# Weights of both output projections and of keys and values, 192 bytes further into their buffers

## The chip, the cores and the metric

The kernel runs on one core of a Trainium2 chip. The metric is the device time of one execution in microseconds. Before the change the median of three runs is 975.04 us (974.99 to 975.18). Engines are called PE (TensorE; PEld is its loading of the stationary operand), DVE (VectorE), ACT (ScalarE), POOL (GpSimd) and SP (SyncE, which issues most DMAs).

## What is computed

A decoder trunk of two layers over 256 tokens of width 2048, all in float32. Layer 0 is a Mamba-2 mixer, layer 1 is attention over a sliding window of 128 tokens with 32 heads, 4 heads of keys and values, and a sink per head. Cut to what matters here:

```python
# layer 0
zxbcdt = x @ w_in                         # 2048 -> 10304 columns
...                                       # conv, silu, state-space scan, gate, rms norm -> y (256 x 4096)
x = layernorm(ALPHA * x + y @ w_out)      # output projection, 4096 -> 2048
# layer 1
kv = x @ kv_w + kv_b                      # 2048 -> 512, keys and values
proj = x @ w_in                           # 2048 -> 4096, queries and gates
...                                       # rotary, scores, softmax with sink, values -> o (256 x 2048)
x = layernorm(ALPHA * x + (o * silu(gate)) @ w_out)   # output projection, 2048 -> 2048
```

## The kernel before

Nearly all of the work is these matrix products, and each weight is used once. Weights come from memory in **units** of 128 x 2048 float32 (1 MB), each as two halves of 1024 columns, through six buffers `wr` (L169). A product in float32 is made of three products in the faster type float32r: ACT copies a half into a high part `wh` (L178), which rounds it, and DVE subtracts that from the original and stores the rest as the low part `wl` (L181). Activations are split in the same way into `xH` and `xL`, `x1H` and `x1L`, `yH` and `yL`, `oH` and `oL`. A product is then high x high + high x low + low x high, three matmuls into the same accumulator.

Units are used in two ways.

- **Narrow** (`narrow`, `q_block`, `gate_block`, through `mac`, L265): the weights are the stationary operand, 128 x 128 at a time, and 256 tokens of activations move. A unit is 16 blocks x 3 = 48 matmuls of 256 columns. The input projection of layer 0 (`in_wa`, 80 units) and the queries and gates of layer 1 (`in_wq`, `in_wg`, 32 units) run so.
- **Wide** (`out_unit`, L339, and `x_stat`, L1052): the activations are the stationary operand, and 512 columns of weights move. A unit is 2 halves of the tokens x 4 blocks x 3 = 24 matmuls of 512 columns. The output projections (`in_wo`, 32 units, and `in_wb`, 16 units) and keys and values (`in_wkv`, 4 units) run so. In the very last unit the second half of the tokens goes in two pieces of 256 columns.

**Where the parts lie in their buffers.** There are four buffers `wh` and four `wl`, each of 2112 float32 a partition: 2048 for the unit, and 64 (256 bytes) to spare. A table of places, `(offset, first block, last block)` in float32, says where in the buffer the 16 blocks stand: `WHOLE` puts all at 0; `BROKEN` and `BROKEN2`, for the queries and gates, put most blocks at a multiple of 256 bytes plus 64, and the first one or two at 0 (`wh`) or 192 (`wl`) bytes. `split_half` writes there, and the matmuls read from there. The activations of layer 0 (`Split`) lie 192 bytes past a multiple of 256, but for their first block; `yH`, `yL`, `x1H`, `x1L`, `oH` and `oL` begin at a multiple of 256 bytes, and so does every 128 x 128 block in them. The program puts each of the buffers named here at an address that is a multiple of 256.

**Order.** `srcs` lists the units in the order of their use: the input blocks of `SEQ`, with units of the output projection let in by `OUT_AT`, then the rest of that projection, keys and values, and the units of `B_ORDER`. `next_unit` loads `AHEAD = 2` units beyond the one in use: SP issues their DMAs as `wr` buffers come free, ACT and DVE split them as `wh` and `wl` buffers come free. Other work of ACT and DVE (convolution, scan, softmax, the evictions of accumulators, L348 and its neighbours) stands between the splits on the same engines.

Of the kernel before, what the change touches and what calls it, by code (L numbers as in the profile page):

```python
# [20 lines left out]
KT = D // P  # L21
# [76 lines left out]
def trunk(ctx: ExitStack, tc: tile.TileContext, A: dict, out: bass.AP, dbg=None):  # L98
# [51 lines left out]

    WHOLE = [(0, 0, KT)]
    BROKEN = [[(0, 0, 1), (144, 1, KT)], [(1968, 0, 1), (16, 1, KT)]]
    BROKEN2 = [[(0, 0, 2), (272, 2, KT)], [(1840, 0, 2), (16, 2, KT)]]

    def new_unit(places):
# [29 lines left out]
    def load_unit(src, places, pin=False, pin_h=False, n=(1, 1)):  # L185
        u = new_unit(places)
        raws = [load_half(u, src, c, n[c]) for c in range(2)]
        for c in range(2):
            split_half(u, raws[c], c, pin, pin_h)
        return u  # L190
# [24 lines left out]


    srcs = []

    def wo_srcs(name, j):
        return [A[name][j * 4 + i] for i in range(4)]  # L220

    for n, (g, b) in enumerate(SEQ):
        srcs.append(A["wa"][g * 10 + (BLOCKS0.index(b) if g == 0 else b)])
        if n in OUT_AT:
            g, i = OUT_AT[n]
            srcs.append(A["wo"][g * 4 + i])
    srcs += [A["wo"][(NG - 2) * 4 + i] for i in (1, 2, 3)]
    srcs += wo_srcs("wo", NG - 1) + [A["wkv"][i] for i in range(4)]
    places = {}
    for what, j in B_ORDER:  # L230
        if what in "gq":

            places.update({len(srcs) + i: BROKEN2 if (what, i, j) == ("g", 1, 0) else BROKEN for i in range(4)})
        srcs += wo_srcs({"q": "wq", "g": "wg", "o": "wb"}[what], j)
# [3 lines left out]
    def load_next(n, pin=False, pin_h=True):  # L238
        for _ in range(n):
            if len(units) == 4:  # L240
                nc.sync.dma_start(cc[:], A["cc"])
            for i in [i for i, n in enumerate(XK_AT) if n == len(units)]:

                v = xr[:, i % 2, i // 2 * 1024 : i // 2 * 1024 + 1024]
                tc.keep_in_program_order(
                    nc.sync.dma_start(v, A["xk"][:, i % 2, i // 2 * 1024 : i // 2 * 1024 + 1024])
                )


            i = len(units)  # L250
            units.append(
                load_unit(
                    srcs[i], places.get(i, [WHOLE, WHOLE]), pin, pin and pin_h,
                    [2 if 2 * i + c >= 2 * len(srcs) - SPLIT else 1 for c in range(2)],
                )
            )

    def next_unit(behind=False):
        load_next(min(used[0] + 1 + AHEAD, len(srcs)) - len(units), behind, not behind)
        used[0] += 1  # L260
        return units[used[0] - 1]
# [535 lines left out]
    first_ps = first_products()  # L797
    dt_first, dt_second = make_dt(first_ps[0])
    load_next(1, True)
    dt_begun = dt_first()  # L800
    load_next(1, True)
    dt_sums = dt_second()
    load_next(1, True)
# [780 lines left out]
```

## Time and profile before

| what | value |
|---|---|
| median of the runs | 975.04 us |
| profiled execution, first to last instruction (its span) | 973.8 us |
| the median's distance to that span | 1.24 us |
| PE busy, matmul records | 965.5 us, 7332 |
| PEld busy | 892.0 us |
| DVE busy | 786.6 us |
| ACT busy | 671.4 us |
| DMA queue of SP, share of the 16 engines' span | 59.1% |
| granted TensorE clock | 1.000 |

The profile gives one time for the profiled execution, its span; the times of the runs include what lies around it. A matmul's record is longer than the spacing of matmuls: a wide one's is 390 ns, a narrow one's 277 ns, and they overlap. What a matmul costs is read from start to start, or from merged runs in the chain of waits (start, length, count). A line of the windows view has a stretch, its length, the busy time of an engine with the number of its instructions, the granted clock, the share of DMA time and the bytes per second.

### The profile page before, as it was taken

Reading aid. Unit: us, or ns where it says so; the run is one execution under the profiler, and the core shown is the slowest. Engines: PE = TensorE matmul, PEld = TensorE weight load, DVE = VectorE, ACT = ScalarE, POOL = GpSimd, SP = SyncE. Lnnn points to the kernel's source line nnn. Section 1 sums busy time; section 2 is a strip of 40 time slices with the busy share of each in tenths; the row PEclk is TensorE's granted clock in tenths of the full one; section 3 lists DMA queues with packets and bytes.
Section 4 is the critical chain, followed back from the end, with each engine's and each line's share of the span. In section 5 each row is a group of like instructions: output and inputs, shape, how many; then the busy total and the mean of one; then the engine's idle time right before and its main releaser. Section 6 shows DMA issues by size and latency. Waiting matters only on the chain.

```text
span 973.8 us, 18857 instructions
## 1 busy us (share of the span) xinstructions
PE 965.5 (99%) x7332; PEld 892.0 (92%) x7332; DVE 786.6 (81%) x1217; ACT 671.4 (69%) x1282; POOL 119.1 (12%) x202
## 2 busy tenths in 40 slices
PE   9999999999999999999999999999999999999998
PEld 8999989998999999999899899888999988898976
DVE  7978898896977877787797687889977769778778
ACT  7675884884785686487477579467777776884772
POOL 0000403102110310310300121411000000000002
PEclk9999999999999999999999999999999999999999
DMA  9689467676656666576476654568654545456542
GB/s 359 237 290 337 147 216 228 212 230 203 218 192 220 205 205 206 167 237 213 152 250 203 216 178 155 187 190 265 193 174 158 185 138 186 153 177 213 205 143 86
DMA packets 61273, 197.90 MB, mean 203 GB/s; under 512 B 6800, under 2 KB 11328, under 8 KB 60928
## 3 DMA queue, kind: packets, MB, share of 16 engines
q1 hardware_dynamic: 58528, 188.53, 59.1%
q0 software_dynamic: 2048, 7.65, 2.4%
q8 instruction: 57, 0.93, 0.4%
q10 hardware_dynamic: 608, 0.52, 0.2%
q14 instruction: 32, 0.26, 0.1%
HBM read 194.45 MB, written 2.23 MB: 202 GB/s over the span
## 4 chain that ended last, share of the span: by engine, by line
PE 75%; DVE 10%; ACT 6%; DMA 5%; issue 3%; SPq 1%; DVEq 0%; ACTq 0%
PE mm L265 48%; PE mm L339 20%; DVE wl L181 4%; DMA wr<-in_wa 2%; PE mm L1052 2%; PE ax L670 2%; ACT wh L178 2%; DMA wr<-in_wb 1%; ACT p L1248 1%; DMA xr<-in_first 1%; DVE cv L510 1%; ACT e L566 1%; ACT ptw L1281 1%; ACT pt L1281 0%; DMA rscr<-f 0%
## 5 line engine op out<-in xcount | busy, mean ns | idle before, releaser
L181 DVE TENSOR_TENSOR wl<-wr,wh 128x1024 fp32r<-128x1024 f32 (+2 forms) x354 | 391.5, 1126 | 87.8 <-ACT wh L178 86.0
L178 ACT ACTIVATE wh<-wr 128x1024 fp32r<-128x1024 f32 (+2 forms) x354 | 332.9, 974 | 95.9 <-PE mm L265 50.9
L265 PE MATMUL mm<-xH,wh 128*128 128x256 f32 x1280 | 354.6, 277 | 0.1
L265 PE MATMUL mm<-xH,wl 128*128 128x256 f32 x1280 | 353.8, 276 | 0.0
L265 PE MATMUL mm<-xL,wh 128*128 128x256 f32 x1280 | 353.7, 276 | 0.0
L265 PEld LDWEIGHTS mm<-xH,wh 128*128 128x128 f32 x1280 | 240.3, 188 | 2.3 <-issue 1.0
L265 PEld LDWEIGHTS mm<-xL,wh 128*128 128x128 f32 x1280 | 240.4, 188 | 1.0
L265 PEld LDWEIGHTS mm<-xH,wl 128*128 128x128 f32 x1280 | 240.3, 188 | 0.1
L265 PE MATMUL mm<-x1H,wh 128*128 128x256 f32 x512 | 142.2, 278 | 2.1 <-DVE sg L1186 2.1
L265 PE MATMUL mm<-x1L,wh 128*128 128x256 f32 x512 | 141.6, 277 | 0.0
L265 PE MATMUL mm<-x1H,wl 128*128 128x256 f32 x512 | 141.5, 276 | 0.0
L339 PE MATMUL mm<-wh,yH 128*128 128x512 f32 x256 | 100.8, 394 | 0.1
L339 PE MATMUL mm<-wh,yL 128*128 128x512 f32 x256 | 99.8, 390 | 0.0
L339 PE MATMUL mm<-wl,yH 128*128 128x512 f32 x256 | 99.7, 390 | 0.0
L265 PEld LDWEIGHTS mm<-x1H,wh 128*128 128x128 f32 x512 | 96.1, 188 | 3.6 <-DVE sg L1186 2.4
L265 PEld LDWEIGHTS mm<-x1L,wh 128*128 128x128 f32 x512 | 96.2, 188 | 0.1
L265 PEld LDWEIGHTS mm<-x1H,wl 128*128 128x128 f32 x512 | 96.2, 188 | 0.0
L510 DVE SCALAR_TENSOR_TENSOR cv<-mm,pc,cv 128x255 f32<-128x255 f32 x144 | 68.4, 476 | 4.6 <-ACT cv L508 2.5
L686 POOL TENSOR_TENSOR yz<-yz,z 128x256 f32<-128x256 f32 x32 | 26.7, 843 | 259.2 <-DVE yz L681 259.2
L339 PEld LDWEIGHTS mm<-wl,yH 128*128 128x128 f32 x256 | 48.1, 188 | 10.3
L339 PEld LDWEIGHTS mm<-wh,yH 128*128 128x128 f32 x256 | 48.1, 188 | 9.7 <-issue 0.3
L339 PEld LDWEIGHTS mm<-wh,yL 128*128 128x128 f32 x256 | 48.1, 188 | 9.0
(247 smaller groups left out, 1262.8 us busy)
## 6 DMA issues: line engine op xcount, KB each, us to landing
wr<-in_wa SPq DMA_DIRECT2D x154, 512.0 KB, 5.2
wr<-in_wo SPq DMA_DIRECT2D x64, 512.0 KB, 4.4
wr<-in_wq SPq DMA_DIRECT2D x32, 512.0 KB, 4.4
wr<-in_wg SPq DMA_DIRECT2D x31, 512.0 KB, 4.8
wr<-in_wb SPq DMA_DIRECT2D x16, 512.0 KB, 4.0
wr<-in_wb SPq DMA_DIRECT2D x32, 256.0 KB, 4.3
rb<-rscr SPq DMA_DIRECT2D x11, 512.0 KB, 5.4
wr<-in_wkv SPq DMA_DIRECT2D x8, 512.0 KB, 5.7
```

What stands on the lines that cost most here:

```text
L178: m = nc.scalar.activation(h[:, sl], v, AF.Copy)
L181: m = nc.vector.tensor_tensor(l[:, sl], v, h[:, sl].bitcast(F32), ALU.subtract)
L265: m = nc.tensor.matmul(ps, a, b, start=first and i == 0, stop=last and i == 2)
L339: pinned(nc.tensor.matmul(ps, a[:, k, hs], (u.h, u.l)[l][:, ks], start=n == 0 and add is None, stop=n == 11), pin)
L510: nc.vector.scalar_tensor_tensor(a[:, sft:], ps[:, : S - sft], w(3 - sft), a[:, sft:], ALU.mult, ALU.add)
L566: m = nc.scalar.activation(e[:, h, cols], rb[:, h, c * P :], AF.Relu, scale=-1.0, bias=rtk[:, c, h0 + h : h0 + h + 1])
L670: nc.tensor.matmul(ps[64 * r : 64 * r + 64, cols], st.xd[:, c, i, 64 * r : 64 * r + 64], e[:, 256:] if c else e[:, :256], start=c == 0, st ...
L686: nc.gpsimd.tensor_tensor(v, v, st.z[i][:], ALU.mult)
L1052: m = nc.tensor.matmul(ps[:], (x1H, x1L, x1H)[i][:, kk, hs], (u.h, u.h, u.l)[i][:, ks], start=(kk, i) == (0, 0), stop=ui == 3 and (k, i) = ...
L1248: nc.scalar.activation(byhead[:, r], byhead[:, r], AF.Exp, bias=ng[:, r : r + 1], accum_out=rs[:, r : r + 1])
L1281: nc.scalar.copy(to[32 * c : 32 * c + 32].rearrange("p r a -> p (r a)"), src[32 * i : 32 * i + 32, cc_].rearrange("p r b -> p (r b)"),)
```

## The change

A new table of places, `ASIDE`, puts all 16 blocks of both parts at offset 48, which is 192 bytes. The loop that lists the units notes in `stood` the positions of the units of the input projection. A unit which is neither noted there nor has a place in `places` (queries and gates) now gets `ASIDE` in place of `WHOLE`: the units of both output projections and of keys and values. 48 + 2048 = 2096 float32 fit into a buffer's 2112. Nothing else is changed; the sequence of instructions on every engine, and what each waits for, is the same in both programs.

```diff
     WHOLE = [(0, 0, KT)]
     BROKEN = [[(0, 0, 1), (144, 1, KT)], [(1968, 0, 1), (16, 1, KT)]]
+    ASIDE = [[(48, 0, KT)], [(48, 0, KT)]]
     BROKEN2 = [[(0, 0, 2), (272, 2, KT)], [(1840, 0, 2), (16, 2, KT)]]
...
     srcs = []
+    stood = set()
...
     for n, (g, b) in enumerate(SEQ):
+        stood.add(len(srcs))
         srcs.append(A["wa"][g * 10 + (BLOCKS0.index(b) if g == 0 else b)])
...
                 load_unit(
-                    srcs[i], places.get(i, [WHOLE, WHOLE]), pin, pin and pin_h,
+                    srcs[i], places.get(i, [WHOLE, WHOLE] if i in stood else ASIDE), pin, pin and pin_h,
                     [2 if 2 * i + c >= 2 * len(srcs) - SPLIT else 1 for c in range(2)],
```

## The prediction

> **What bounds the kernel now.** I read the head of the page first, then its chain of work that ended last.
>
> ```profile
> span 973.8 us, 18857 instructions
> PE 965.5 (99%) x7332; PEld 892.0 (92%) x7332; DVE 786.6 (81%) x1217; ACT 671.4 (69%) x1282; POOL 119.1 (12%) x202
> PE 75%; DVE 10%; ACT 6%; DMA 5%; issue 3%; SPq 1%; DVEq 0%; ACTq 0%
> ```
>
> PE's 99% says little, because matmul records overlap. The third line says more: for three quarters of the span the chain runs through PE itself. The question is therefore what one matmul costs PE, and where in the program PE sets the pace.
>
> The change touches only "wide" matmuls: a stationary block of activations (128x128) and 512 columns of weights as the moving operand. They stand at L339 (both output projections) and L1052 (keys and values). The windows view, restricted to L339, counts them by stretch (columns: stretch, its length, PE busy and the number of matmuls, granted clock, DMA share, GB/s); the last row is the same view for L1052 over the whole span.
>
> ```profile
> 0.00:130.40 130.40, 11.34 (x48) 1.00 0.77 269
> 130.40:784.00 653.60, 168.89 (x720) 1.00 0.63 202
> 784.00:835.60 51.60, 22.59 (x96) 1.00 0.51 160
> 835.60:900.00 64.40, 22.24 (x96) 1.00 0.58 187
> 900.00:953.00 53.00, 32.93 (x140) 1.00 0.46 160
> 953.00:973.80 20.80, 12.42 (x64) 1.00 0.27 101
> 0.00:973.80 973.80, 22.28 (x96) 1.00 0.62 203
> ```
>
> That is 1164 + 96 = 1260 wide matmuls, all at a granted clock of 1.00. I cut the stretches where the chain changes hands. The chain view's summary line for each of the first five stretches, in order:
>
> ```profile
> by line: DMA wr<-in_wa 17.1%; DVE wl L181 15.2%; issue 11.7%; DMA xr<-in_first 6.3%; DVE cv L510 5.7%; ACT e L566 5.2%; ACT wh L178 3.9%; DMA rscr<-f 3.6%; SPq L206 3.5%; ACT e L573 3.2%; DVE yz L681 3.0%; DVE yL L701 2.1%; DVE e L614 1.6%;
> by line: PE mm L265 66.0%; PE mm L339 25.2%; PE mm L1052 3.3%; PE ax L670 2.9%; PE ax L607 0.5%; PE ax L983 0.5%; PE ax L1220 0.4%; PE ax L1213 0.3%; PE ax L608 0.2%; PE mm L1342 0.2%; PE ax L1328 0.2%; PE mm L1349 0.1%; DVE z L600 0.1%; AC
> by line: DVE wl L181 16.6%; issue 13.8%; ACT p L1248 11.1%; ACT wh L178 8.2%; ACT ptw L1281 7.9%; DVE xr L346 4.8%; DVE sm L1242 4.4%; ACT pte L1281 2.9%; DVE z L1262 2.9%; DVE sw L1151 2.9%; DVE o L1316 2.5%; DVE qT L1154 2.4%; DVE oL L135
> by line: PE mm L265 60.2%; PE mm L339 34.2%; PE ax L1213 1.7%; PE mm L1328 1.6%; PE ax L1342 1.3%; PE ax L1349 0.9%; issue 0.1%
> by line: DMA wr<-in_wb 20.5%; DVE wl L181 18.5%; issue 14.7%; ACT wh L178 11.6%; ACT pt L1281 6.9%; ACT p L1248 5.4%; DVE z L1262 4.7%; DVE xr L350 3.4%; DVE p L1255 2.4%; ACT p L1233 2.2%; ACT ptw L1281 1.5%; DVE sg L1186 1.3%; DVE st L946
> ```
>
> In the second and fourth stretch nothing but PE stands in the chain; a nanosecond taken off a matmul there comes off the span. In the first, third and fifth the chain goes through DVE, ACT and loads while PE keeps just ahead of them; PE time saved there turns into a wait. After 953 us the chain is PE again, until the last matmul:
>
> ```profile
> 953.05 10.82 PE mm L339 x52
> ```
>
> **What a matmul costs, and what address has to do with it.** All times below are from start to start, since the record of one matmul (about 390 ns for a wide one) covers the next one's beginning. I call "distance" the byte address at which the moving operand begins, minus that of the stationary one, modulo 256. Every buffer that these matmuls read begins at a multiple of 256 bytes, so distances follow from the offsets in the code: 0 for all wide matmuls now (weights at 0, activations at 0), 192 for the narrow matmuls (256 columns) of L265, in the first layer because the activations lie 192 bytes in, in the second because the weights lie 64 bytes in (0 - 64 = 192). Merged runs in the chain view (start, length, count):
>
> ```profile
> 349.09 5.45 PE mm L339 x24
> 354.54 10.91 PE mm L265 x96
> 321.86 27.23 PE mm L265 x240
> 677.56 38.19 PE mm L265 x336
> ```
>
> A wide matmul takes 5.45 / 24 = 227 ns. A narrow one takes 27.23 / 240 = 113.5 ns in the first layer and 38.19 / 336 = 113.7 ns in the second. Half the columns take half the time, so this alone could be a plain rate, with nothing to gain. The end of the kernel decides against that: there L339 itself runs pieces of 256 columns, still at distance 0. From the timeline of PE:
>
> ```profile
> 955.25 0.39 PE L339 MATMUL mm<-wl,oH 128*128 128x512 f32 x1
> ...
> 962.05 0.39 PE L339 MATMUL mm<-wl,oH 128*128 128x512 f32 x1
> ...
> 963.95 0.28 PE L339 MATMUL mm<-wh,oH 128*128 128x256 f32 x1
> ...
> 965.27 0.28 PE L339 MATMUL mm<-wl,oH 128*128 128x256 f32 x1
> ```
>
> Wide: 31 matmuls, 30 intervals in 6.80 us, 226.7 ns each. Pieces of 256 at distance 0: 12 matmuls, 11 intervals in 1.32 us, 120.0 ns each, 6.5 ns more than the narrow ones at distance 192. So 256 further columns cost 226.7 - 120.0 = 106.7 ns, and each matmul has a fixed part of 120.0 - 106.7 = 13.3 ns at distance 0. At distance 192 the fixed part is 113.5 - 106.7 = 6.8 ns. The same step shows once more where a unit of the second layer begins: its first products stand at distance 0 or 64, the later ones at 192.
>
> ```profile
> 677.40 0.28 PE L265 MATMUL mm<-x1H,wh 128*128 128x256 f32 x1
> 677.51 0.28 PE L265 MATMUL mm<-x1L,wh 128*128 128x256 f32 x1
> 677.64 0.28 PE L265 MATMUL mm<-x1H,wl 128*128 128x256 f32 x1
> 677.75 0.28 PE L265 MATMUL mm<-x1H,wh 128*128 128x256 f32 x1
> ```
>
> These three take 350 ns together, 117 each, against the 113.7 above. I read it this way: while one matmul streams, PE already loads the next stationary block, both read the same partitions, and when their addresses run along together one of them is held up.
>
> [...]
>
> **The change, part by part.** The order of instructions on all five engines, and what each waits for, is the same before and after; no instruction, DMA or wait is added or taken away, so there is no queue to go past. What differs, in 52 units of weights (32 and 16 of the two output projections, 4 of keys and values), is where ACT (L178) and DVE (L181) write the two parts, and where PE reads them.
>
> - The split on ACT and DVE: the groups view by shape has 896-column pieces, written 64 bytes in, beside whole halves of 1024, of which nine in ten are written at 0.
>
> ```profile
> L181 DVE TENSOR_TENSOR wl<-wr,wh 128x1024 fp32r<-128x1024 f32 x290 | 350.0, 1224 | 74.5 <-ACT wh L178 72.8
> L181 DVE TENSOR_TENSOR wl<-wr,wh 128x896 fp32r<-128x896 f32 x31 | 33.6, 1083 | 3.1 <-ACT wh L178 3.0
> L178 ACT ACTIVATE wh<-wr 128x896 fp32r<-128x896 f32 x31 | 29.2, 942 | 0.0
> ```
>
>  1083 / 896 = 1.21 and 1224 / 1024 = 1.20 ns a column on DVE: no cost of the place is to be seen. I put it at nothing. If a wide unit's split did get slower, its cover is PE's 24 matmuls, 5.45 us a unit, against two DVE splits of 1.22 us; in the third and fifth stretch there is no cover and each 0.1 us would show.
> - The wide matmuls: their distance becomes 192, that of the narrow ones. I expect the fixed part to fall from 13.3 to 6.8 ns, 6.5 ns a matmul, 226.7 to 220.2 ns. Nothing in the trace has 512 columns at distance 192, so this is carried over from 256. The bounds: no gain, if in a wide matmul the loading has so much time that it gives way (0), and 13.3 ns, if the whole fixed part goes. I take 6.5 because distance 0 cost the 256- and the 512-column matmuls of L339 the same fixed 13.3 ns, so length does not seem to matter.
> - What of it reaches the end: 720 + 96 + 96 + 64 = 976 matmuls stand on PE's chain (second and fourth stretch, L1052, the end), 976 x 6.5 = 6.3 us. The other 284 (48 + 96 + 140) would save 1.8 us, which I count as lost: in the third stretch PE ends up waiting for DVE anyway,
>
> ```profile
> 835.64 0.39 PE L265 MATMUL mm<-x1H,wh 128*128 128x256 f32 x1 [2.07 <-DVE sg L1186]
> ```
>
>  and saving 96 x 6.5 = 0.6 us there makes these 2.07 us longer. If all were kept, the gain would be 8.2 us.
> - Entering and leaving wide units: PE's rhythm changes over a few matmuls. On entry, from the timeline:
>
> ```profile
> 381.65 0.39 PE L339 MATMUL mm<-wh,yH 128*128 128x512 f32 x1
> 381.88 0.40 PE L339 MATMUL mm<-wh,yL 128*128 128x512 f32 x1
> 382.11 0.39 PE L339 MATMUL mm<-wl,yH 128*128 128x512 f32 x1
> 382.34 0.39 PE L339 MATMUL mm<-wh,yH 128*128 128x512 f32 x1
> ```
>
>  690 ns for three, 10 above three times 226.7. After a wide unit the run at 354.54 took 10.91 / 96 = 113.65 ns a matmul, 0.15 x 96 = 14 ns above the long run's rate. Some 30 blocks of wide work have both edges: 30 x 24 ns = 0.7 us, which may go or double. I take 0 and keep 0.7 us on both sides.
> - Covers: a faster unit asks for 1 MB of weights in 24 x 220.2 = 5.28 us in place of 5.44. ACT and DVE each hold two splits for it and DVE two evictions besides (745 ns each by the row below), 2 x 1.22 + 2 x 0.75 = 3.9 us, and the DMA share in that stretch is 0.63. Nothing there becomes the bound.
>
> ```profile
> L348 DVE SCALAR_TENSOR_TENSOR xr<-mm,r,xr 128x512 f32<-128x512 f32 x64 | 47.0, 745 | 9.7 <-POOL r L744 4.8 <-PE mm L339 4.7 <-ACT r L742 0.3
> ```
>
> Sum: 973.8 - 6.3 = 967.5 us for the profiled span. The median of the runs, 975.04, is 1.24 us above that execution's span; with the same 1.24 the forecast is **968.7 us**. With the edges and with all or fewer of the matmuls counted, this case's own range is 966.2 (975.0 - 8.2 - 0.7, rounded) to 970.7.
>
> **The rivals.**
>
> *No change, 975.0.* In a wide matmul the stationary load has 227 ns for a job that the narrow ones do in 113; it could simply give way at a collision, and what costs a wide matmul its 13.3 ns could be something that the address does not touch. For it: half the columns at distance 192 take exactly half the time, which a plain rate would explain too, with the 120.0 ns a matter of short matmuls alone. Against it: the coincidence of 13.3 ns would then be chance.
>
> *Slower, 981.3.* Two readers that run at different speeds can lock into a worse rhythm as well as a better one. That a wide matmul can be slower than 226.7 ns is in the rows at 381.65: 230 ns each right after a narrow unit. If the offset that suits 256 columns leaves the two out of step at 512, so that the stream is held up once more for each stationary load, at the price of one such hold-up above (6.5 ns), the 976 matmuls on PE's chain cost 6.3 us: 975.0 + 6.3 = 981.3. The place is every wide unit; it decides from the point at which the fixed part at distance 192 is above 13.3 ns. Against it: at 256 columns the same two distances go the other way, in thousands of narrow matmuls.
>
> *Much faster, 962.0.* The whole fixed part goes: 13.3 x 976 = 13.0 us. For it speaks only that the narrow 6.8 ns could be bound by the load and not by the stream, and in a wide matmul the load has time. [...]
>
> **How the numbers follow.** Forecast 0.62, no change 0.21, slower 0.12, much faster 0.05. A measurement of this kernel tells about 0.2% from nothing, 1.95 us; forecast and much faster are both beyond it, so faster 0.67, same 0.21, slower 0.12. The range goes from 966.0 to 975.3: it holds the forecast's own 966.2 to 970.7 and the case of no change, and leaves out the slower case and the much faster one, 0.17.
>
> **What would show it.** In the profile of the changed kernel: merged runs of L339 x24 at 5.28 us in place of 5.45; the 256-column pieces at the end at 113.5 in place of 120.0 ns; L265 runs, and the means of L178 and L181, as before; the wait at L265 for DVE (2.07 us) longer by some 0.6 us and new waits of PE in the third and fifth stretch. The forecast is wrong if wide runs stay at 5.45 us (no change), if they grow (slower), or if they shrink and the span does not, which would put a load or a split at the end of the second stretch's chain.

## The result and the profile after

| | before | changed | ratio |
|---|---|---|---|
| median of the runs | 975.11 us (974.99 to 975.46, 4 runs) | 986.89 us (986.02 to 987.3, 4 runs) | 1.0118 [1.0104, 1.0133] |
| span of the profiled execution | 973.8 us | 985.5 us | |

The change costs 11.8 us; the forecast was a gain of 6.3 us. The edits add three lines, so L265 is now L268, L339 is L342, L1052 is L1055, and L178 and L181 are L179 and L182.

The page of the changed kernel, its head and the first line of its chain of waits:

```profile
span 985.5 us, 18857 instructions
PE 978.2 (99%) x7332; PEld 900.1 (91%) x7332; DVE 788.2 (80%) x1217; ACT 671.9 (68%) x1282; POOL 119.3 (12%) x202
PE 94%; DVE 3%; ACT 2%; issue 1%; DVEq 0%; ACTq 0%
```

The instructions are the same in number, and DVE, ACT and POOL work as long as before (786.6, 671.4 and 119.1 us there); the time is PE's, whose share of the chain of the whole span goes from 75% to 94%.

The chain view of the changed kernel at the beginning of the second stretch (start, length, what, count), to be held against the prediction's rows of 5.45, 10.91 and 27.23 us:

```profile
144.81 5.79 PE mm L342 x24
150.60 28.27 PE mm L268 x240
178.87 0.43 PE ax L610 x2
...
179.52 10.90 PE mm L268 x96
190.43 5.59 PE mm L342 x24
196.02 11.31 PE mm L268 x96
...
238.88 0.22 PE ax L611 x2
239.10 5.60 PE mm L342 x24
244.71 27.21 PE mm L268 x240
```

Two things got slower. A wide unit takes 5.60 us in place of 5.46: from start to start its matmuls are 233.3 ns apart, where they were 226.7. And narrow units, which the change doesn't touch, are slower too, but not all: the row at 196.02 has 117.8 ns a matmul, the one at 179.52 has 113.5. The slow ones stand behind a wide unit and stay slow, five units long in the row at 150.60, until PE does something else (L610, L673) or another wide unit comes. Of the 77 units of the input projection that run one after the other (the first three of the 80 are interleaved), 34 go at 117.8 ns; before it was none. Of the 32 units of queries and gates it is one before and two after.

This accounts for the time. Two rows of the kernel before mark the second stretch, from the first wide unit that stands in its chain to its end:

```profile
144.77 5.66 PE mm L339 x24
...
783.94 0.38 ACT pt L1281
```

and one of the changed kernel marks the same end:

```profile
795.09 0.40 ACT pt L1284
```

From the one row to the other it grew from 639.17 to 650.28 us, by 11.1. In it stand 33 wide units, 0.14 us more each (4.6), and 32 slow narrow units, 0.205 us more each (11.31 - 10.90 for two; 6.6): 11.2 together. The third stretch ends where PE's wait for DVE ends:

```profile
846.79 0.39 PE L268 MATMUL mm<-x1H,wh 128*128 128x256 f32 x1 [1.82 <-DVE sg L1189]
```

It is 51.70 us long, as before (795.09 to 846.79 against 783.94 to 835.64); PE's wait there went from 2.07 to 1.82 us. The rest went from 138.2 to 138.7.

The splits, in the groups view by shape (busy us, mean ns of one, then idle time), the second row from the kernel before:

```profile
L182 DVE TENSOR_TENSOR wl<-wr,wh 128x1024 fp32r<-128x1024 f32 x290 | 350.3, 1225 | 84.3 <-ACT wh L179 82.7
L178 ACT ACTIVATE wh<-wr 128x1024 fp32r<-128x1024 f32 x290 | 297.7, 1051 | 82.1 <-PE mm L265 45.0 <-PE mm L339 16.4 <-issue 10.7
L179 ACT ACTIVATE wh<-wr 128x1024 fp32r<-128x1024 f32 x290 | 297.9, 1051 | 96.0 <-PE mm L268 52.7 <-PE mm L342 23.0 <-issue 13.2
```

1225 ns against 1224 on DVE, and 1051 against 1051 on ACT. Some 104 of these 290 halves were moved (52 units of two halves), so 1 ns in the mean is at most some 3 ns for a moved one: writing at another place costs ACT and DVE nothing that can be seen. (The pieces of 896 columns that the prediction named belong to queries and gates, which stay where they were.)

The 256-column pieces of the last unit, from the timeline: the second and last matmul of the first piece, and the first and last of the second.

```profile
974.22 0.28 PE L342 MATMUL mm<-wh,oL 128*128 128x256 f32 x1
...
975.36 0.28 PE L342 MATMUL mm<-wl,oH 128*128 128x256 f32 x1
...
975.70 0.28 PE L342 MATMUL mm<-wh,oH 128*128 128x256 f32 x1
...
976.99 0.28 PE L342 MATMUL mm<-wl,oH 128*128 128x256 f32 x1
```

Ten intervals in 1.14 us, 114 ns, and eleven in 1.29 us, 117.3 ns. The same instruction at the same distance runs at two spacings within 3 us.

The two spacings are not new with the change either. Among the first units of the program, ahead of every wide unit, where the two programs run the same matmuls at the same places, 48 matmuls take 5.44 us in the kernel before (13.36 to 18.80, 113.3 ns each) and 5.66 us in the changed one (13.75 to 19.41, 117.9 ns). Of the eight profiles of whole kernels in this case three have the first spacing there and five the second.

### The profile page after: what moved, and what is told of

Its sections match the earlier page's. It is cut to its first block, busy times and chain, and to the rows that moved or that the text cites. A ratio compares the mean times of both kernels' runs of the same rounds, so it can differ in the third digit from the quotient of the medians.

```text
span 985.5 us, 18857 instructions
## 1 busy us (share of the span) xinstructions
PE 978.2 (99%) x7332; PEld 900.1 (91%) x7332; DVE 788.2 (80%) x1217; ACT 671.9 (68%) x1282; POOL 119.3 (12%) x202
## 3 DMA queue, kind: packets, MB, share of 16 engines
q0 software_dynamic: 2048, 7.65, 2.5%
## 4 chain that ended last, share of the span: by engine, by line
PE 94%; DVE 3%; ACT 2%; issue 1%; DVEq 0%; ACTq 0%
PE mm L268 61%; PE mm L342 25%; PE mm L1055 2%; PE ax L673 2%; DVE wl L182 1%; ACT p L1251 1%; PE ax L610 0%; PE mm L409 0%; ACT wh L179 0%; PE ax L1223 0%; ACT ptw L1284 0%; PE ax L986 0%; PE ax L1216 0%; PE ax L391 0%; DVE t L1419 0%
## 5 line engine op out<-in xcount | busy, mean ns | idle before, releaser
L182 DVE TENSOR_TENSOR wl<-wr,wh 128x1024 fp32r<-128x1024 f32 (+2 forms) x354 | 391.9, 1128 | 98.0 <-ACT wh L179 96.2
L179 ACT ACTIVATE wh<-wr 128x1024 fp32r<-128x1024 f32 (+2 forms) x354 | 333.3, 974 | 111.1 <-PE mm L268 58.6
L268 PE MATMUL mm<-xH,wh 128*128 128x256 f32 x1280 | 357.6, 279 | 0.0
L268 PE MATMUL mm<-xL,wh 128*128 128x256 f32 x1280 | 356.7, 279 | 0.0
L268 PE MATMUL mm<-xH,wl 128*128 128x256 f32 x1280 | 356.5, 279 | 0.0
L268 PEld LDWEIGHTS mm<-xH,wh 128*128 128x128 f32 x1280 | 242.9, 190 | 2.0 <-ACT wh L213 0.3
L268 PEld LDWEIGHTS mm<-xL,wh 128*128 128x128 f32 x1280 | 240.5, 188 | 1.2
L268 PEld LDWEIGHTS mm<-xH,wl 128*128 128x128 f32 x1280 | 240.5, 188 | 0.0
L268 PE MATMUL mm<-x1H,wh 128*128 128x256 f32 x512 | 142.4, 278 | 1.8 <-DVE sg L1189 1.8
L268 PE MATMUL mm<-x1L,wh 128*128 128x256 f32 x512 | 141.8, 277 | 0.0
L268 PE MATMUL mm<-x1H,wl 128*128 128x256 f32 x512 | 141.6, 277 | 0.0
L342 PE MATMUL mm<-wh,yH 128*128 128x512 f32 x256 | 102.1, 399 | 0.0
L342 PE MATMUL mm<-wl,yH 128*128 128x512 f32 x256 | 101.2, 395 | 0.0
L342 PE MATMUL mm<-wh,yL 128*128 128x512 f32 x256 | 101.2, 395 | 0.0
L268 PEld LDWEIGHTS mm<-x1H,wh 128*128 128x128 f32 x512 | 96.1, 188 | 3.4 <-DVE sg L1189 2.2
L268 PEld LDWEIGHTS mm<-x1L,wh 128*128 128x128 f32 x512 | 96.3, 188 | 0.1
L268 PEld LDWEIGHTS mm<-x1H,wl 128*128 128x128 f32 x512 | 96.2, 188 | 0.0
L342 PEld LDWEIGHTS mm<-wl,yH 128*128 128x128 f32 x256 | 48.1, 188 | 11.6
L342 PEld LDWEIGHTS mm<-wh,yH 128*128 128x128 f32 x256 | 48.2, 188 | 10.7 <-DVE wl L182 0.2
L342 PEld LDWEIGHTS mm<-wh,yL 128*128 128x128 f32 x256 | 48.2, 188 | 10.3
```

Of the source, the lines that this page charges most:

```text
L179: m = nc.scalar.activation(h[:, sl], v, AF.Copy)
L182: m = nc.vector.tensor_tensor(l[:, sl], v, h[:, sl].bitcast(F32), ALU.subtract)
L268: m = nc.tensor.matmul(ps, a, b, start=first and i == 0, stop=last and i == 2)
L342: pinned(nc.tensor.matmul(ps, a[:, k, hs], (u.h, u.l)[l][:, ks], start=n == 0 and add is None, stop=n == 11), pin)
```

## The experiments

The theories after the result: the spacing depends on the **distance** (1); it depends on the **place** of the weights alone (2); or PE is disturbed by **ACT and DVE**, which write next to what it reads (3). Beside that, the two parts of the loss had to be told apart, and the narrow units explained.

In the small programs below, which run PE alone, a section is mostly 36 or 48 matmuls in the kernel's order of products. Each program was executed once, and its granted clock was 0.998 to 1.000. A spacing is read from start to start after the first few; the chain's rows, which are shown, hold those first ones too.

### Every distance, PE alone

```diff
+SECTIONS = [("w" + LET[i], 512, 16 * i, 0, 36, True) for i in range(16)]
+SECTIONS += [("n" + LET[i], 256, 16 * i, 0, 48, True) for i in range(16)]
+# then: both operands at 192; the stationary one alone at 192;
+# 24 wide matmuls at 0, 64, 128 or 192 and, right behind, 96 narrow ones at 192
```

> This kernel leaves the model out: PE alone runs rows of matmuls on constant data, and nothing else works meanwhile. 512 columns and 256 columns, with the moving operand 0, 16, 32, ... 240 bytes past a multiple of 256 and the stationary one at 0; then both operands moved by 192, then only the stationary one; then 24 wide matmuls at 0, 64, 128 or 192 followed without a break by 96 narrow ones at 192. Theory 1 (PE's spacing is set by the distance between its two operands, and by the length): 512 columns take 226.7 ns at 0 and 233.5 at 192, 256 columns 120.0 at 0 and 113.3 at 192, both moved is as at 0. Theory 2 (the place of the moving operand alone): both moved is as 192. Theory 3 (it comes from what ACT and DVE do in the changed places): 512 columns take 226.7 at every distance here. On what follows: if PE carries its rhythm on, narrow ones after wide ones at 0 take 113.3 and after wide ones at 192 117.8; if not, all four take 113.3.

From the chain view (w is 512 columns, n is 256; the second letter is the distance, a = 0, e = 64, i = 128, m = 192; "both" and "stat" are as in the edit; "then" follows its "lead" without a break):

```profile
51.20 8.26 PE we L66 x36
121.59 8.41 PE wm L66 x36
157.09 5.75 PE na L66 x48
230.48 5.47 PE nm L66 x48
254.74 8.19 PE bothw L66 x36
263.37 4.30 PE bothn L66 x36
268.11 8.26 PE statw L66 x36
276.80 4.25 PE statn L66 x36
281.48 5.49 PE leada L66 x24
286.97 11.31 PE thena L66 x96
...
332.90 5.60 PE leadm L66 x24
338.51 10.90 PE thenm L66 x96
```

| columns | 0 | 64 | 128 | 192 | the other twelve distances |
|---|---|---|---|---|---|
| 512, ns | 226.7 | 228.9 | 232.5 | 233.3 | 231.1 to 236.7 |
| 256, ns | 120.0 | 117.8 | 118.6 | 113.3 | 113.3 (at 112) to 120.1 |

With nothing running on the other engines the 233.3 ns of the changed kernel are back, so ACT and DVE are not the cause. Both operands moved by 192 give 226.7 and 120.0, as at 0; the stationary one alone moved by 192 gives 228.9 and 117.8, as at 64 (0 - 192 = 64). So it is the distance, not the place. And what is best for 256 columns, 192, is among the bad ones for 512, where 0 is best.

The last four rows show the second effect without the kernel: the same 96 narrow matmuls at distance 192 take 117.8 ns behind wide ones at 0 and 113.5 behind wide ones at 192. (At 64 it was 117.8, at 128 113.5.) They have two rhythms, and keep the one into which they were started. That something is carried over was expected, but the other way round: 113.3 behind 0 and 117.8 behind 192, as in the kernel. There a narrow unit begins with products at 0 and 64, here it begins at 192, and the third and the last experiment test whether that is the difference.

### Only the units behind the last narrow one

```diff
-[WHOLE, WHOLE] if i in stood else ASIDE
+[WHOLE, WHOLE] if i in stood or i < tail else ASIDE   # tail: end of the input projection
```

> Only the 27 wide units behind the last unit of the input projection are moved (the last 7 of the first output projection, keys and values, the second output projection); the other 25 stay at 0. Theory 1 (wide matmuls at 192 cost 6.9 ns more each, and narrow units of the first layer that come behind them cost 4.5 ns a matmul): no narrow unit is slowed here, 424 matmuls on PE's chain x 6.9 = 2.9 us, up to 648 x 6.9 = 4.5: 978.0 to 979.6, and all narrow units at 113.3. Rival (the loss is spread over the program, as by the split on ACT and DVE or by memory): half of the 11.8 us, 981.

Measured: 977.39 us (976.61 to 979.71, 10 runs) beside 975.13 (19 runs), ratio 1.0024 [1.0014, 1.0033]. In its chain view a wide unit that stays at 0, the narrow run behind it, and a wide run that was moved:

```profile
348.14 5.46 PE mm L343 x24
353.60 10.90 PE mm L269 x96
...
869.36 16.79 PE mm L343 x72
```

The moved ones take 233.2 ns, the others 226.7 ns, and no unit of the input projection is slow. The loss, 2.3 us, is under the 2.9 to 4.5 that were expected. Of the 27 units 11 stand in the second stretch and cost 1.6 us there (from the first of them to the next narrow unit 65.7 us, from 612.50 to 678.22, against 64.1 before), and some 50 matmuls at the very end cost 0.3; of the other units' loss little reaches the end, as PE waits there anyway: in the kernel before 2.07 us at L265 for DVE, and from 900 to 953 us PEld at L339 waits 1.6 us for the splits of L181.

### The change, with another entry into the narrow units

A narrow unit behind other work reads its first block of activations from a place at 0 (high) or 64 (low); within a run it reads a copy at 192 (`steady`). The edit takes the copy behind wide units as well.

```diff
             out_units(g, [i])
-            steady[0] = False
+            steady[0] = True
```

> As the change, but the first narrow unit behind a wide one reads its first block of activations from the copy at 192 bytes, so that it begins at distance 192 as it goes on. If the way a narrow unit begins decides which rhythm it keeps: the units at 117.8 go back to 113.3 and 5 to 6 us of the 11.8 come back, 981. If the wide unit ahead decides: the same time as the change, 986.9, with the units at 117.8 where they are.

Measured: 981.01 us (979.97 to 982.24, 4 runs), ratio 1.0056 [1.0037, 1.0074]. Chain view:

```profile
189.94 5.59 PE mm L342 x24
195.54 10.89 PE mm L268 x96
```

Wide units are as slow as in the change, and narrow ones as fast as before, but for 3 of 77: those behind the first three wide units, which also begin at 192, stay at 117.8 ns, and why is open. Three products at the start of a unit decide the spacing of the 45 that follow: 96 matmuls behind a wide unit take 10.89 us, where they took 11.31. It also halves the 11.8 us: 5.9 (986.89 - 981.01) for the narrow units, 5.9 for the wide ones. By the profiled spans it is 6.5 (985.5 - 979.0) and 5.2 (979.0 - 973.8), nearer to the sums above.

### 64 bytes in place of 192

```diff
-    ASIDE = [[(48, 0, KT)], [(48, 0, KT)]]
+    ASIDE = [[(16, 0, KT)], [(16, 0, KT)]]
```

> As the change, but 64 bytes in place of 192. If the place by itself costs (any shift off 0): 987. If the distance sets it, another value: 512 columns at distance 64 as in the map of e1, anywhere from 220 to 240 ns, so 1260 x the difference to 226.7, plus what narrow units behind them lose.

Measured: 978.07 us (976.89 to 979.03, 10 runs), ratio 1.0026 [1.0017, 1.0035]. Chain view:

```profile
188.64 5.50 PE mm L342 x24
194.15 10.92 PE mm L268 x96
```

A wide unit takes 5.50 us (228.9 ns a matmul, as the first experiment has for 64), and none of the 77 units of the input projection is caught; four of the 32 of queries and gates are, where it was one before. 1260 x 2.2 ns = 2.8 us, and the loss is 2.9 (978.07 - 975.13): the time goes by the size of the step that PE alone shows, and not by the mere fact of a shift.

### High and low parts at places of their own, PE alone

The four parts (high and low, moving and stationary) at 0, 64, 128 or 192 bytes each, 64 combinations for each length:

```diff
+for i in range(64):
+    x, y, z = i // 16, i // 4 % 4, i % 4
+    SECTIONS.append(("w" + LET[x] + LET[y] + LET[z], 512, 64 * x, 64 * y, 0, 64 * z, 36))
+    # and the same for "n" with 256 columns
```

> The model is left out again; PE alone. Each of the four parts (high and low of the moving operand, low of the stationary one, against the high stationary one at 0) is put at 0, 64, 128 or 192 bytes, 64 combinations for 512 columns and 64 for 256. All at 0: 226.7 and 120.0 ns; both moving parts at 192: 233.5 and 113.3; both at 64: 228.9 and 117.8, as in the first map. If each matmul only cares for its own distance, a combination's mean lies between those of its members, nothing at 512 columns is below 226.7 and nothing at 256 below 113.3. If the rhythm is made by all three matmuls of a step together, some combinations lie outside of these, and one below 226.7 would make a faster kernel.

Chain view (letters: high moving, low moving, low stationary part; a, b, c, d = 0, 64, 128, 192; high stationary at 0):

```profile
437.01 8.43 PE wdaa L62 x36
...
577.59 5.75 PE naaa L62 x48
944.47 5.46 PE ndda L62 x48
```

For 512 columns only all four at 0 gives 226.7; the other 63 lie from 228.9 to 234.4. For 256 columns two combinations give 113.3, the kernel's ndda (both moving parts at 192) and one more; the rest goes up to 121.1. So no place of a part is better than the kernel before has it. Nor does each matmul care for its own distance alone: the three of wdaa stand at 192, 192 and 0, which by themselves give 233.3 and 226.7, and together they take 234.4. The rhythm is made by all three of a step. The values are not spread evenly: for more than half of the wide and of the narrow combinations (46 and 39 of 64 by one way of averaging; others differ by some), a step of three matmuls lies within 0.4 ns of a whole multiple of 6.67 ns (680.0 = 102 x 6.67, 686.7 = 103, 693.3 = 104, 700.0 = 105), where an even spread would give 8 of 64. At the prediction's 106.7 ns for 256 columns, 6.67 ns is the time of 16 columns (64 bytes), an estimate.

### Other lengths, PE alone

```diff
+for d in (0, 64, 192):
+    for i, n in enumerate(range(256, 513, 32)):
+        SECTIONS.append(("l" + LET[d // 64] + LET[i], n, d, d, 0, 0, 36))
```

> PE alone, the model left out. First the length: 256, 288, ... 512 columns at distance 0, 64 and 192. What the prediction assumed: the fixed part (spacing less 0.4167 ns a column) is the same at every length, 13.3 ns at distance 0 and 6.7 at 192. What the result suggests: at distance 0 it is 13.3 at 256 and at 512, at 192 it goes from 6.7 at 256 to 20 at 512, so that somewhere between the two distances change places. Then the 64 combinations of places as before, with the second and third product of a step exchanged, for 512 and for 256 columns. If the order inside a step is indifferent: 226.7 and 113.3 stay the smallest. If a rhythm below 226.7 exists in this order, it is a faster kernel.

Fixed part of a matmul, in the prediction's terms: its spacing less 0.4167 ns a column (106.7 / 256).

| columns | 256 | 288 | 320 | 352 | 384 | 416 | 448 | 480 | 512 |
|---|---|---|---|---|---|---|---|---|---|
| distance 0, ns | 13.3 | 11.7 | 13.3 | 14.4 | 13.3 | 15.0 | 16.0 | 16.7 | 13.3 |
| distance 64, ns | 11.1 | 11.7 | 13.3 | 13.3 | 13.3 | 15.0 | 13.3 | 18.3 | 15.6 |
| distance 192, ns | 11.1 | 13.3 | 13.3 | 13.3 | 16.7 | 13.3 | 15.5 | 16.0 | 20.0 |

(The 13.3 at 256 columns and distance 0 is the first experiment's 120.0. In this program's order of products, that of the wide units, 256 columns at 192 came to 117.8, the slower of the two rhythms.) Rows of distance 192 (second letter d; the third counts the lengths from 256 up, i is 512):

```profile
137.42 4.24 PE lda L66 x36
...
159.26 6.37 PE lde L66 x36
...
189.17 8.41 PE ldi L66 x36
```

The fixed part isn't a property of the distance: at 192 it goes from 11.1 through 13.3, 16.7 and 13.3 again to 20.0 as the matmul grows, and at 0 it is as low at 512 columns as at 384. Length and distance decide together. The 106.7 ns were worked out from two lengths that were taken to have the same fixed part; the difference between two rows at one length needs no such figure, and from distance 0 to 192 it goes from -2.2 at 256 columns through +3.4 at 384 and -1.7 at 416 to +6.7 at 512. The two distances change places more than once. That is the step that the prediction lacked.

The 64 combinations with the second and third product exchanged (the wide ones here in the order of the narrow, and the reverse):

```profile
894.68 5.47 PE nbbc L66 x48
...
1126.81 5.66 PE ndda L66 x48
```

Again only all four at 0 gives 226.7 for 512 columns, the others up to 235.6, and 113.3 is the least for 256: no faster kernel here. But the two places that give 113.3 are not the same two. The kernel's ndda takes 117.8 in this order, and nbbc, which took 118.9, takes 113.3. So the order inside a step counts as well.

### The 32 units of the first output projection, and their activations with them

Here only the units of `in_wo` move, and in the second kernel `yH` and `yL` also begin 192 bytes further, so that the distance is 0 again while the weights lie where the change puts them. The first edit is common, the second is the second kernel's alone:

```diff
-[WHOLE, WHOLE] if i in stood else ASIDE
+[WHOLE, WHOLE] if i in stood or i >= first else ASIDE   # first: end of in_wo
```
```diff
-                yp.tile([P, 4, S], F32R, tag="yH", name=nm("yH"), bufs=2),
-                yp.tile([P, 4, S], F32R, tag="yL", name=nm("yL"), bufs=2),
+                yp.tile([P, 4 * S + 64], F32R, tag=n, name=nm(n), bufs=2)[:, 48 : 48 + 4 * S].rearrange("p (i s) -> p i s", s=S)
+                for n in ("yH", "yL")
```

> Only the 32 wide units of the first output projection are moved by 192 bytes. If distance and carried rhythm are the cause: wide units of this projection at 233, most narrow units behind them at 117.8, and nearly all of the loss, as the other 20 units cost 256 matmuls on PE's chain x 6.9 = 1.8 us: 985.

> As the run beside it (the units of the first output projection moved by 192 bytes), and the activations that they meet, the high and low parts of y, moved by 192 bytes too: ACT and DVE write all of these in the changed places and PE reads them there, but the distance between PE's two operands is 0 again. If the distance decides: wide units back at 226.7, no narrow unit kept at 117.8, 975. If the place decides (where ACT and DVE write, where PE reads): 985, as without the second move.

Measured: weights alone 986.17 us (985.45 to 986.51, 4 runs), ratio 1.0112 [1.0095, 1.0129]; weights and activations 975.37 (974.47 to 976.42, 10 runs), ratio 1.0001 [0.9992, 1.0011]. The chain views, first of weights alone, then of both:

```profile
189.85 5.59 PE mm L344 x24
195.45 11.31 PE mm L270 x96
```

```profile
188.07 5.46 PE mm L344 x24
193.54 10.90 PE mm L270 x96
```

With weights alone 34 of 77 narrow units run at 117.8 ns, with both none. The whole loss goes when the distance goes back to 0, with the weights still at 192 (975.37 beside 975.47 us). In the kernel itself too it is the distance, and the place of what ACT and DVE write has no part in it.

### The kernel before, with the other entry alone

If narrow units carry over a rhythm, the kernel before must be one edit away from the same loss, with no weight moved: by the first experiment, wide units at 0 with an entry at 192 give 117.8 ns.

```diff
             out_units(g, [i])
-            steady[0] = False
+            steady[0] = True
```

> The kernel before, all weights where they were, with the one edit of e3: the first narrow unit behind a wide one begins at the copy at 192 bytes. In the map of e1 narrow matmuls at 192 that follow wide ones at 0 without a break kept 117.8 ns, those behind wide ones at 192 took 113.3. If a rhythm is carried from wide to narrow in the model as it is there: wide units stay at 226.7, some 30 narrow units go to 117.8, 0.2 us each, and the kernel is 5 to 7 us slower, 980 to 982, though no wide matmul has changed. If only the wide units' own place costs narrow ones their time: 975, all narrow units at 113.3.

Measured: 987.13 us (986.85 to 987.49, 4 runs), ratio 1.0126 [1.0109, 1.0142]. Chain view:

```profile
189.59 5.46 PE mm L339 x24
195.05 11.31 PE mm L265 x96
...
243.29 28.27 PE mm L265 x240
```

Wide units are as fast as before, and yet the loss is that of the whole change: 61 of 77 narrow units run at 117.8 ns, 61 x 0.205 = 12.5 us. Expected were some 30 units, since the change itself caught 34. The 26 units of five long runs make up all but one of the difference: in the change they keep 113.4 ns (the row at 244.71), behind a wide unit that itself stands directly behind L611, and here they are caught (the row at 243.29). The edit that repairs half of the loss when the wide units lie at 192 makes as large a loss when they lie at 0.

| wide units at | first narrow products at | narrow spacing, ns | seen in |
|---|---|---|---|
| 0 | 0 and 64 | 113.3 | kernel before |
| 0 | 192 | 117.8 | PE alone; kernel before with the other entry |
| 64 | 0 and 64 | 113.3 | 64 in place of 192 |
| 64 | 192 | 117.8 | PE alone |
| 192 | 0 and 64 | 117.8; 113.3 behind L611 | the change |
| 192 | 192 | 113.3, but for 3 units | PE alone; the change with the other entry |

The column of spacings is that of the input projection.

## Why the prediction was wrong

**The wide matmuls: the step that failed.** The fixed part was to fall from 13.3 to 6.8 ns "because distance 0 cost the 256- and the 512-column matmuls of L339 the same fixed 13.3 ns, so length does not seem to matter". It rose to 20.0 ns (233.3 - 213.3). That both lengths have 13.3 at distance 0 was chance: between them it goes from 11.7 to 16.7, and at 192 it differs by 8.9 ns or more between 256 and 512 columns. The bounds were drawn around the same assumption, from 0 to 13.3 ns of gain, and allowed no loss, although the prediction had said itself that no row showed 512 columns at 192. Nor were the 6.5 ns the price of the distance alone at 256 columns: they were the difference to one of two spacings at 192, and against the other, 117.8, which PE alone showed in the wide units' own order of products, it is 2.2. This term was put at -6.3 us and measured +5.2 by the spans and +5.9 by the medians (the third experiment, where it stands almost alone).

**Entering and leaving wide units: the second.** It was taken as 0 with 0.7 us on both sides, an edge of a few matmuls. The edge decided how the whole run behind it went: 0.205 us for each of 32 units, +6.6 us in the second stretch. The row at 354.54, an unaltered run behind a wide unit, showed only that the old edge was harmless.

**The rival "slower", 981.3.** It had the sign and, for the wide matmuls alone, the size: 981.01 in the third experiment. Of its mechanism the runs show that "the offset that suits 256 columns" doesn't suit 512, and at 192 a loss of the size that it took (20.0 - 13.3 = 6.7 ns). That this is one hold-up more per stationary load isn't shown: other distances cost from 2.2 (at 64) to 10.0 ns (at 240), so that the price fits may be luck. It lacked the narrow units, and so half of the loss.

**No change.** The 120.0 ns at distance 0 beside the 113.5 at 192 were read rightly: addresses do matter. With no engine but PE at work, the spacing of 512 columns went from 226.7 to 236.7 ns by the distance alone (the first experiment). **Much faster** falls with the first step: no combination of places gave 512 columns less than 226.7, in either order of the products.

**What held.** The distance as the variable, by the two kernels that move weights alone and weights with activations, though not the distance alone. The count of 1260 (24 of them are the pieces of 256 columns). The splits at no cost (1224 and 1225 ns on DVE, 1051 and 1051 on ACT). The stretches: the second passed everything on, and the third none of its wide matmuls' loss, 51.70 us before and after, though as a wait that became 0.25 us shorter, since PE came later, and not 0.6 longer. The first of the 256-column pieces at the end at 114 ns; the second was at 117.3, the other rhythm.

**What stays open.** Why 512 columns at distance 192 settle at 233.3 ns and at 0 at 226.7; why the five long runs behind L611 escaped in the change, and three units were caught with the other entry; what set the spacing of the first units of the program, which changes from profile to profile; and what in PE waits, and for what: that the loading of the stationary block and the stream hold each other up is the prediction's reading of 120.0 against 113.5 ns, and no run shows it.

## What to carry to other kernels

A spacing measured for one length of matmul said nothing certain here about another length at the same addresses (from distance 0 to 192, 256 columns went from 120.0 to 113.3 ns and 512 from 226.7 to 233.3): measure the pair of length and distance that is to be used, with PE alone, before moving buffers. When an edit changes the rhythm of some matmuls, read the unedited ones behind them as well, run by run and not by their mean; here they were half of the loss (5.9 of 11.8 us), and three products at the start of a run decided 45 to 285 that followed. Move both operands together if a buffer must move: with the weights alone moved the kernel took 986.17 us, with their activations moved too 975.37.

## What the runs showed of the hardware that was not expected

- Two steady spacings of the same matmuls at the same addresses, 113.3 and 117.8 ns, chosen in the runs above by the wide unit ahead together with the first three products, and kept over as many as 288 matmuls until PE did other work. On the kernel before, one edit of the entry is worth 12.3 us (974.81 to 987.13).
- The spacing of matmuls with 512 columns goes from 226.7 to 236.7 ns with the distance, that of 256 columns from 113.3 to 120.1, and the two lengths don't agree on a good distance.
- More than half of the steady spacings (46 of 64 wide and 39 of 64 narrow combinations) make three matmuls, one step of high and low parts, within 0.4 ns a whole number of 6.67 ns.
